# One SBUF layout for all layers of a two-layer decoder trunk, and output projections that take half of their k-tiles by seven-product blocks

## The chip, the cores and the metric

The kernel runs on one core of a Trainium2 chip. The core has a matrix engine (TensorE, PE in the profile, with PEld for its weight loads), a vector engine (VectorE, DVE), an activation engine (ScalarE, ACT), GpSimd (POOL), and SyncE (SP), whose queue issues the weight loads from device memory. On-chip memory is SBUF, 128 partitions wide; TensorE writes its sums to PSUM, eight banks of 512 float32 columns per partition.

The metric is the device time of one execution in microseconds, the median of several runs. Less is better.

## The reference

The program computes a decoder trunk of two layers on 256 positions and a width of 2048, all in float32:

```
def reference(x, ...):
    for layer in range(2):
        h = rms_norm(x, mix_norm[layer])
        if layer is even:
            z, xbc, dt_raw, c_q, c_kv, k_rope = split(h @ w_in)
            y_ssd = ssd_mixer(...)      # state space, 32 heads of 64, norm with a gate silu(z)
            y_mla = mla_mixer(...)      # latent attention, 16 heads of 128
            mix = concat(y_ssd, y_mla) @ w_out_even        # (4096, 2048)
        else:
            q, k, v = split(h @ w_qkv)
            mix = stick_breaking(q, k, v) @ w_out_odd      # (2048, 2048), 16 heads of 128
        x = x + mix
        h = rms_norm(x, ffn_norm[layer])
        x = x + (silu(h @ w_gate) * (h @ w_up)) @ w_down   # hidden width 5632
    return rms_norm(x, final_norm)
```

What matters here are the three square projections of 2048 to 2048 that write into the residual `x`: the upper half of `w_out_even` (from the state-space heads), its lower half (from the latent attention heads, MLA), and `w_out_odd` (from the stick-breaking heads).

## The kernel before, in words

**Products.** A float32 number is split in two parts, hi (a cast to the matrix engine's float32r) and lo (the rest). A product of two matrices is three matmuls: hi by hi, lo by hi, hi by lo. The cast is ACT's (`split`, L251), the subtraction that leaves lo is DVE's (L252). Each weight is loaded once into a tile of 4 k-tiles by 512 columns (1 MB), and split into two tiles wh and wl, called parts here.

**Plain projections.** `project` walks through the k-tiles of one block of 512 output columns; for each k-tile there are 3 matmuls for each of the two halves of the 256 positions (L345 to L347). A block over 16 k-tiles is 96 matmuls of 128x512. Two PSUM banks take the sums, and the next block uses the other two.

**Seven-product pairs.** `pair` computes two blocks at once: the gate's and the up-projection's 512 columns in the feed-forward stage. Its first 8 k-tiles form a 2x2 block product (two halves of the positions by two halves of k on one side, two halves of k by two column blocks on the other), taken by seven products in place of eight, after Winograd. A product is 12 matmuls (L499, L500, L504), so the phase of seven products has 84. The other 8 k-tiles are done in the plain way (96 matmuls, L532 to L534). For the seven products the weights are added to each other first (`wadd`, L470), and so are the activations (`block_operands`, L434, L447 and L448), once for a stage. In the text w11, w22, w21 are the splits of loaded weights, and wt1 to wt4 those of the four sums t1 to t4. The products use, in this order, w11, w22, wt1, w21, wt2, wt4, wt3. The lo part of a weight is used in the last four of the 12 matmuls only. DVE takes two more subtractions of the partial results (L515).

**Memory.** SBUF holds a pool of 42 tiles for activations (`s2`), three weight tiles, and one shared region that is laid out in two ways. In a mixing layer (`acts`) it holds 20 further activation tiles (`s2x`) and four parts each of wh and wl of two k-tiles. In a feed-forward stage (`sums`) it holds a fourth weight tile, three parts each of wh and wl of four k-tiles, and two tiles for sums. `region` changes from one to the other between the stages.

**Order.** The order of PE's instructions is written out by hand. Beside the projections stand small tasks (generators, `spawn`), which go on after so many ticks; a tick is one k-tile of a projection, or a half of a product. The heads of the attention, the state-space groups, transposes and the activations' splits are such tasks; `join` runs a task to its end where its result is needed. DVE, ACT, POOL and SP are put in order by a scheduler, by priority among what it holds to be ready: weight loads, weight splits and weight sums have priorities that count up from 100000, urgent work has 50000, and the rest, at 10000000 and up, comes last.

The even layer runs: the convolution's input projections with the state-space groups beside them, the latent projections, four blocks of the gate z, four MLA groups, then the state-space half of the output projection, then MLA's half. The odd layer runs four groups of stick-breaking heads, then its output projection.

Of the kernel before, what the change touches and what calls it, by code (L numbers as in the profile page):

```python
# [8 lines left out]
F32 = mybir.dt.float32  # L9
# [6 lines left out]
P = 128  # L16
D = 2048
KD = D // P
# [9 lines left out]
class Trunk:  # L28
# [6 lines left out]
    def __init__(self, ctx, tc, ins, out):  # L35
# [5 lines left out]
        self.ap = ec(tc.tile_pool(name="acts", bufs=42))  # L41
# [4 lines left out]
        self.shared, self.shared_kind = None, None  # L46
        self.region("acts")
        ctx.callback(self.region, None)
        self.banks = ["acc0", "acc1", "acc2", "acc3"]
        self.n = self.wn = 0  # L50
# [37 lines left out]
    def region(self, kind):  # L88


        if self.shared is not None:
            self.shared.__exit__(None, None, None)
        self.shared, self.shared_kind = None, kind
        if kind:
            self.shared = self.tc.tile_pool(name=f"shared_{kind}", bufs=2, reuse_waits="tile")
            self.xp = self.shared.__enter__()

    def s2x(self, shape, dt=F32):

        return self.xp.tile([P, *shape], dt, name=self.nm("s2x"), tag="s2x", bufs=20)  # L100
# [12 lines left out]
    def wsum(self):  # L113
        return self.xp.tile([P, 4, 512], F32, name=self.nm("wsum"), tag="wsum", bufs=2)
# [27 lines left out]
    def constants(self):  # L142
# [14 lines left out]
        with self.priority(self.wprio + 6500):  # L157
            self.wdt = []
            for q in range(4):
                w = self.s2x([4, 96])  # L160
# [141 lines left out]
    def load_split(self, view, nk, n):  # L302

        nc = self.nc
        for k0 in range(0, nk, 4):
            k1 = min(nk, k0 + 4)
            res = []
            with self.priority(self.wprio):
# [7 lines left out]
                np = 2 if self.shared_kind == "acts" else 4  # L316
                for a in range(k0, k1, np):
                    b = min(k1, a + np)
                    wh, wl = self.part("wh"), self.part("wl")
                    step = 1 if self.wprio < 102000 else np  # L320
                    for c in range(0, b - a, step):
                        d = min(c + step, b - a)
                        self.split(wh[:, c:d, :n], wl[:, c:d, :n], w[:, a - k0 + c:a - k0 + d, :n])
                    for k in range(a, b):
                        res.append((wh[:, k - a, :n], wl[:, k - a, :n]))
# [58 lines left out]

    def norm_begin(self):
        return {"ssq": self.small([P, 2, 4], "ssq"), "xT": [], "A": [], "S": []}
# [8 lines left out]
    def add_residual(self, ps, j, scale=None):  # L395
        nc, x = self.nc, self.xres
        for t in range(2):
            xs = x[:, t, j * 512:(j + 1) * 512]
            with self.priority(self.URGENT):
                if scale is None:  # L400
                    nc.vector.tensor_tensor(xs, ps[t], xs, op=ALU.add)
                else:
                    nc.vector.scalar_tensor_tensor(xs, ps[t], scale[:, t:t + 1], xs, op0=ALU.mult, op1=ALU.add)
# [4 lines left out]
    def operand_block(self, st, j, g):  # L408

        nc, x = self.nc, self.xres

        def gen():
            for t in range(2):
                yield 2 if t == 0 else 1
                pt = self.tr([4, P])
                for k in range(4):
                    nc.tensor.transpose(pt[:, k], x[:, t, j * 512 + k * P:j * 512 + (k + 1) * P], self.ident)
                r = self.s2([4, P])  # L420
                nc.vector.tensor_tensor(r, pt, g[:, 4 * j:4 * j + 4].unsqueeze(2).to_broadcast([P, 4, P]),
                                        op=ALU.mult)
                st["A"].append(r)
            for t in range(2):
                self.square_sum(x[:, t, j * 512:(j + 1) * 512], st["ssq"][:, t, j:j + 1])
            if j == 1:
                yield 1
                st["S"].extend(self.block_operands(*st["A"]))
        st["xT"].append((self.spawn(gen()), None))

    def block_operands(self, a11, a21, a12, a22):

        nc = self.nc
        sub = lambda o, p, q: nc.vector.tensor_tensor(o, p, q, op=ALU.subtract)  # L434
        d1, d2, d4 = (self.s2([4, P]) for _ in range(3))
        sub(d1, a21, a22)
        sub(d2, a11, d1)
        sub(a21, a21, a11)
        sub(d4, a12, d2)
        res = []  # L440
        for n, a in enumerate((a11, a12, a22, d1, d2, a21, d4)):
            hi, lo = self.s2([4, P], F32R), self.s2([4, P], F32R)
            if n == 0:
                nc.scalar.activation(hi, a, AF.Copy, scale=-1.0)
                nc.vector.scalar_tensor_tensor(lo, a, -1.0, hi.bitcast(F32), op0=ALU.mult, op1=ALU.subtract)
            else:
                nc.scalar.copy(hi, a)  # L447
                nc.vector.tensor_tensor(lo, a, hi.bitcast(F32), op=ALU.subtract)  # L448
            res.append((hi, lo))
        return res  # L450
# [16 lines left out]
    def wadd(self, o, p, q):  # L467
        with self.priority(self.wprio):
            self.wprio += 100
            self.nc.vector.tensor_tensor(o, p, q, op=ALU.add)  # L470
        return o

    def pair(self, st, xT, va, vb, left, right):
# [3 lines left out]
        mm = nc.tensor.matmul  # L477
        b11, b12 = self.wload(va, 0), self.wload(vb, 0)
# [77 lines left out]
    def ffn(self, layer, st, gain_next):  # L556
        nc, i = self.nc, self.i
        wg, wu, wd = i["w_gate"][layer], i["w_up"][layer], i["w_down"][layer]
        self.region("sums")
        xT, rstd = self.pairs(st["xT"]), None  # L560
        h = [None, None]

        def left(t, c, s):
# [3 lines left out]
            nc.vector.tensor_tensor(s, c, s, op=ALU.subtract)  # L567
# [9 lines left out]
        for nb in (2, 2, 2, 2, 3):  # L577
            act = []
            for n in range(n0, n0 + nb):
                self.pair(st, xT, self.cols(wg, n * 512), self.cols(wu, n * 512), left, right)  # L580
# [16 lines left out]
        if gain_next is not None:  # L597
            self.region("acts")
# [42 lines left out]
    def stick(self, st):  # L641
        nc, i = self.nc, self.i
        wq = i["w_qkv"][0]
        oT, xT, rstd = [], self.pairs(st["xT"]), None
        for g in range(4):
# [13 lines left out]
            oT.append((self.spawn(self.stick_out(v, ws, wts, res)), res))  # L659
        aT = self.pairs(oT)  # L660
        st = self.norm_begin()
        for n in range(4):
            ps = self.project(aT, self.cols(i["w_out_odd"][0], n * 512), KD)
            self.add_residual(ps, n)
            if n < 2:
                self.operand_block(st, n, self.g_ffn[1])
            else:
# [471 lines left out]
```

## Time and profile before

| what | value |
|---|---|
| median of 3 runs | 2493.59 us (2492.51 to 2496.81) |
| profiled execution | 2491.61 us, of which the span is 2489.9 us |
| PE busy | 2438.8 us (98%) |
| DVE busy | 1739.2 us (70%) |
| ACT busy | 1324.8 us (53%) |
| POOL busy | 127.7 us (5%) |

A line of the page or of a view names the line of the program, the engine, the operation, what it writes and reads, and the shapes. A group's line ends with busy time, the mean duration in ns, and the idle time of the engine before these instructions with what ended it. A line of the waits has the total, how often, and the longest. A line of the timeline has start and duration, and in brackets the idle time ahead of it. A line of the windows has a stretch from and to, its length, the busy time of PE, PEld, DVE, ACT and POOL (each with its number of instructions), the granted clock of PE, the share of the DMA engines, and GB/s. Matmuls overlap, so the duration of one (some 390 ns) isn't the step from one to the next.

### The profile page before, as it was taken

The page shows a single profiled execution, that of the slowest core. Times are in us where ns is not written, and L with a number is a line of the kernel's source. Part 1 is how long each engine was busy: PE and PEld are TensorE (multiplying, and loading weights), DVE is VectorE, ACT ScalarE, POOL GpSimd, SP SyncE. Part 2 cuts the span into 40 slices and gives each one's busy share as a digit, 9 for nine tenths or more (in the row PEclk, how much of TensorE's full clock was granted, in tenths as well). Part 3 has the DMA queues.
Part 4 walks back from the last instruction along what each step waited for, and adds up shares of the span by engine and source line. Part 5 has one row for each costly group of instructions (what it writes and reads, how often), then busy time and mean ns, then how long its engine had stood idle before and what let it go on. Part 6 is the DMA issues. An engine that isn't in the chain of part 4 may idle for free.

```text
span 2489.9 us, 28071 instructions
## 1 busy us (share of the span) xinstructions
PE 2438.8 (98%) x11176; PEld 2008.5 (81%) x11176; DVE 1739.2 (70%) x1631; ACT 1324.8 (53%) x1421; POOL 127.7 (5%) x165
## 2 busy tenths in 40 slices
PE   8989999999899999999999999999999999999998
PEld 7777887788778888888878888888778888888877
DVE  6776555546777878787984555556777878787874
ACT  6655555434554545454654456564554545554553
POOL 1342121000000000000000000000000000000001
PEclk9999999999999999999999999999999999999999
DMA  7554553355465656565654555555555656565653
GB/s 236 187 168 136 183 163 111 119 186 186 168 215 175 220 177 224 174 209 196 204 202 152 183 161 163 169 170 184 178 195 184 217 173 221 170 234 170 237 188 117
DMA packets 257828, 454.81 MB, mean 183 GB/s; under 512 B 20716, under 2 KB 45424, under 8 KB 257696
## 3 DMA queue, kind: packets, MB, share of 16 engines
q1 hardware_dynamic: 255168, 446.48, 54.3%
q0 software_dynamic: 1952, 5.48, 0.7%
q8 instruction: 88, 1.44, 0.2%
q10 hardware_dynamic: 576, 1.05, 0.1%
q14 instruction: 44, 0.36, 0.0%
HBM read 450.85 MB, written 2.13 MB: 182 GB/s over the span
## 4 chain that ended last, share of the span: by engine, by line
PE 60%; issue 34%; DVE 3%; POOL 1%; DMA 1%; ACT 1%; SPq 0%; POOLq 0%; ACTq 0%; DVEq 0%
PE acc L345 13%; PE acc L347 13%; PE acc L346 13%; PE acc L532 3%; PE acc L534 3%; PE acc L533 3%; PE acc L499 2%; PE acc L500 2%; PE acc L504 2%; DVE wl L252 1%; PE tr L261 1%; PE at L1062 1%; POOL s L967 1%; ACT wh L251 1%; PE at L991 1%
## 5 line engine op out<-in xcount | busy, mean ns | idle before, releaser
L252 DVE TENSOR_TENSOR wl<-w,wh 128x1024 fp32r<-128x1024 f32 (+2 forms) x586 | 997.7, 1709 | 553.1 <-ACT wh L251 549.1
L251 ACT CAST wh<-w 128x1024 fp32r<-128x1024 f32 (+2 forms) x586 | 837.1, 1430 | 788.2 <-PE acc L347 531.9
L345 PE MATMUL acc<-wh,s 128*128 128x512 f32 (+1 forms) x1728 | 692.2, 401 | 0.6 <-ACT wh L251 0.6
L346 PE MATMUL acc<-wl,s 128*128 128x512 f32 (+1 forms) x1728 | 671.5, 389 | 1.8 <-DVE wl L252 1.7
L347 PE MATMUL acc<-wh,s 128*128 128x512 f32 (+1 forms) x1728 | 672.4, 389 | 0.0
L347 PEld LDWEIGHTS acc<-wh,s 128*128 128x128 f32 x1728 | 325.4, 188 | 68.9
L346 PEld LDWEIGHTS acc<-wl,s 128*128 128x128 f32 x1728 | 326.5, 189 | 66.0 <-DVE wl L252 2.8
L345 PEld LDWEIGHTS acc<-wh,s 128*128 128x128 f32 x1728 | 326.4, 189 | 63.6 <-issue 2.4
L534 PE MATMUL acc<-wl,s 128*128 128x512 f32 x704 | 274.1, 389 | 0.0
L532 PE MATMUL acc<-wh,s 128*128 128x512 f32 x704 | 273.9, 389 | 0.0
L533 PE MATMUL acc<-wh,s 128*128 128x512 f32 x704 | 273.9, 389 | 0.0
L499 PE MATMUL acc<-wh,s 128*128 128x512 f32 x616 | 245.4, 398 | 0.0
L500 PE MATMUL acc<-wh,s 128*128 128x512 f32 x616 | 242.2, 393 | 0.0
L504 PE MATMUL acc<-wl,s 128*128 128x512 f32 x616 | 166.9, 393 | 12.3 <-DVE wl L252 12.3
L251 ACT CAST wh<-wsum 128x2048 fp32r<-128x2048 f32 x66 | 126.4, 1915 | 87.3 <-PE acc L533 33.7
L252 DVE TENSOR_TENSOR wl<-wsum,wh 128x2048 fp32r<-128x2048 f32 x66 | 150.7, 2286 | 13.5 <-ACT wh L251 13.5
L534 PEld LDWEIGHTS acc<-wl,s 128*128 128x128 f32 x704 | 132.1, 188 | 28.2 <-DVE wl L252 0.8
L533 PEld LDWEIGHTS acc<-wh,s 128*128 128x128 f32 x704 | 132.1, 188 | 27.4
L532 PEld LDWEIGHTS acc<-wh,s 128*128 128x128 f32 x704 | 132.1, 188 | 27.4
L504 PEld LDWEIGHTS acc<-wl,s 128*128 128x128 f32 x616 | 115.7, 189 | 39.2 <-DVE wl L252 15.3
L499 PEld LDWEIGHTS acc<-wh,s 128*128 128x128 f32 x616 | 117.8, 191 | 23.6
L500 PEld LDWEIGHTS acc<-wh,s 128*128 128x128 f32 x616 | 117.4, 191 | 23.5
(247 smaller groups left out, 2057.8 us busy)
## 6 DMA issues: line engine op xcount, KB each, us to landing
w<-in_w_gate_dram SPq DMA_DIRECT2D x88, 1024.0 KB, 5.1
w<-in_w_up_dram SPq DMA_DIRECT2D x88, 1024.0 KB, 5.1
w<-in_w_down_dram SPq DMA_DIRECT2D x88, 1024.0 KB, 5.0
w<-in_w_qkv_dram SPq DMA_DIRECT2D x48, 1024.0 KB, 5.0
w<-in_w_in_dram SPq DMA_DIRECT2D x47, 1024.0 KB, 5.1
w<-in_w_out_even_dram SPq DMA_DIRECT2D x32, 1024.0 KB, 4.9
w<-in_w_out_odd_dram SPq DMA_DIRECT2D x16, 1024.0 KB, 4.9
w<-in_w_ukv_dram SPq DMA_DIRECT2D x32, 256.0 KB, 3.8
```

Source lines behind the costliest of these rows:

```text
L251: nc.scalar.copy(hi, src)
L252: nc.vector.tensor_tensor(lo, src, hi.bitcast(F32), op=ALU.subtract)
L261: self.nc.tensor.transpose(pt[:, k, t * P:(t + 1) * P], src(t, 2 * k2 + k), self.ident)
L345: nc.tensor.matmul(ps[t], hi[:, ts], wh, start=k == 0, stop=False)
L346: nc.tensor.matmul(ps[t], hi[:, ts], wl, start=False, stop=False)
L347: nc.tensor.matmul(ps[t], lo[:, ts], wh, start=False, stop=k == nk - 1)
L499: mm(ps, hi[:, k], wh[:, k], start=start and k == 0, stop=False, skip_group_check=True)
L500: mm(ps, lo[:, k], wh[:, k], start=False, stop=False, skip_group_check=True)
L504: mm(ps, hi[:, k], wl[:, k], start=False, stop=k == 3, skip_group_check=True)
L532: mm(ps, hi, wh, start=False, stop=False, skip_group_check=True)
L533: mm(ps, lo, wh, start=False, stop=False, skip_group_check=True)
L534: mm(ps, hi, wl, start=False, stop=stop, skip_group_check=True)
```

## The change

All layers use one layout of SBUF: 46 activation tiles, four weight tiles, three parts each of wh and wl of four k-tiles, and one tile for sums. `region`, `s2x` and the two-k-tile parts go.

With one tile for sums, `pair` writes the sums t1, t2 and t4 into the same tile, each after the one before it has been split; the signs of the sums are another choice, which needs no negated activations.

The three output projections go through `pair` (`project_residual`): two pairs of column blocks for each. Their first 8 k-tiles (two groups of heads) are kept as plain tiles and become the seven operands (`operand_ready`); the other two groups are split as before.

In the even layer the state-space half of the output projection comes ahead of the MLA groups, not behind them. The state-space task waits 6 ticks in place of 3 ahead of the matmul of the chunk's state.

```diff
-        self.ap = ec(tc.tile_pool(name="acts", bufs=42))
+        self.ap = ec(tc.tile_pool(name="acts", bufs=46))
...
-    def wtile(self):
-        self.wn += 1
-        pool, bufs = (self.xp, 1) if self.shared_kind == "sums" and self.wn % 4 == 0 else (self.wp, 3)
-        return pool.tile([P, 4, 512], F32, name=self.nm("w"), tag="w", bufs=bufs)
+    def wtile(self, tag="w", dt=F32, bufs=4):
+        return self.wp.tile([P, 4, 512], dt, name=self.nm(tag), tag=tag, bufs=bufs)
...
     def part(self, tag):
-        nk, bufs = (2, 4) if self.shared_kind == "acts" else (4, 3)
-        return self.xp.tile([P, nk, 512], F32R, name=self.nm(tag), tag=tag, bufs=bufs)
-
-    def wsum(self):
-        return self.xp.tile([P, 4, 512], F32, name=self.nm("wsum"), tag="wsum", bufs=2)
+        return self.wtile(tag, F32R, 3)
...
+    def project_residual(self, st, view, scale=None, done=None):
+        def add(n):
+            def take(t, c, s):
+                if s is not None:
+                    nc.vector.tensor_tensor(s, c, s, op=ALU.add)
+                    c = s
+                self.add_tile(t, c, n, scale() if scale else None)
+            return take
+        for n in (0, 2):
+            self.pair(st, view(n), view(n + 1), add(n), add(n + 1))
+            if done:
+                done(n)
+                done(n + 1)
...
+    def operand_ready(self, st, j, res):
+        nc = self.nc
+        st["A"][j] = res
+        if len(st["A"]) < 2:
+            return
+        (a11, a21), (a12, a22) = st["A"][0], st["A"][1]
+        s1, s2, s4 = (self.s2([4, P]) for _ in range(3))
+        sub = lambda o, p, q: nc.vector.tensor_tensor(o, p, q, op=ALU.subtract)
+        nc.vector.tensor_tensor(s1, a21, a22, op=ALU.add)
+        sub(s2, s1, a11)
+        sub(a21, a11, a21)
+        sub(s4, a12, s2)
+        for a in (a11, a12, a22, s1, s2, a21, s4):
+            hi, lo = self.s2([4, P], F32R), self.s2([4, P], F32R)
+            self.split(hi, lo, a)
+            st["S"].append((hi, lo))
...
-        t1 = self.wadd(self.wsum(), b11, b12)
+        t = self.wtile("wsum", bufs=1)
+        self.wsub(t, b12, b11)
         w11 = self.wsplit(b11)
-        t2 = self.wadd(self.wsum(), t1, b22)
-        t3 = self.wadd(b12, b12, b22)
         w22 = self.wsplit(b22)
-        wt1 = self.wsplit(t1)
-        t4 = self.wadd(self.wsum(), t2, b21)
+        wt1 = self.wsplit(t)
+        self.wsub(t, b22, t)
         w21 = self.wsplit(b21)
-        wt2, wt4, wt3 = self.wsplit(t2), self.wsplit(t4), self.wsplit(t3)
+        self.wsub(b12, b22, b12)
+        wt2 = self.wsplit(t)
+        self.wsub(t, b21, t)
+        wt4, wt3 = self.wsplit(t), self.wsplit(b12)
...
-        for n in range(4):
-            ps = self.project(aT, self.cols(i["w_out_odd"][0], n * 512), KD)
-            self.add_residual(ps, n)
+        self.project_residual(oT, lambda n: self.cols(i["w_out_odd"][0], n * 512), None,
+                              lambda n: self.norm_next(st, n, self.g_ffn[1]))
...
+    def out_tiles(self, g):
+        if g < 2:
+            return [self.s2([4, P]) for _ in range(2)]
+        return [(self.s2([2, S], F32R), self.s2([2, S], F32R)) for _ in range(2)]
...
+        wo = i["w_out_even"][0]
+        self.project_residual(uT, lambda n: self.cols(wo, n * 512), lambda: r_u)
+        oT = self.operand()
         for g in range(4):
             self.mla_group(g, self.pairs(cT[:1]), self.pairs(cT[1:]), oT)
...
-        yield 3
+        yield 6
         pst = self.at([512])
```

More of the change, by code (lines that the diff above doesn't have):

```diff
@@ L418, in gen @@
                 for k in range(4):
-                    nc.tensor.transpose(pt[:, k], x[:, t, j * 512 + k * P:j * 512 + (k + 1) * P], self.ident)
+                    nc.tensor.transpose(pt[:, k], src(t, k), self.ident)
                 r = self.s2([4, P])
[L421 to L425, printed above, removed]
@@ L558, in ffn @@
         wg, wu, wd = i["w_gate"][layer], i["w_up"][layer], i["w_down"][layer]
-        self.region("sums")
-        xT, rstd = self.pairs(st["xT"]), None
+        rstd = None
         h = [None, None]
@@ L1019, in mla_group, with done @@
         v = self.evac(self.project(ckv, heads(wkv, 128, 128), 4))
-        o = [(self.s2x([2, S], F32R), self.s2x([2, S], F32R)) for _ in range(2)]
-        tasks = [self.spawn(self.mla_head(h, qp, q, k, v, o, 2 + 4 * h)) for h in range(4)]
-        oT.append((self.spawn(self.wait_all(tasks)), o))
+        o, left = self.out_tiles(g), [0, 1, 2, 3]
+        def done(h):
+            left.remove(h)
+            if g < 2 and not left:
+                self.operand_ready(oT, g, o)
+        tasks = [self.spawn(self.mla_head(h, qp, q, k, v, g, o, 2 + 4 * h, done)) for h in range(4)]
+        oT["xT"].append((self.spawn(self.wait_all(tasks)), o))
     def wait_all(self, tasks):
```

171 lines of the change are left out of this document (76 added, 95 removed).

## The prediction

> **What bounds the kernel now.** I read the page's first part, the waits of PE, the windows of the seven-product blocks, and the timeline of one of them.
>
> ```profile
> span 2489.9 us, 28071 instructions
> PE 2438.8 (98%) x11176; PEld 2008.5 (81%) x11176; DVE 1739.2 (70%) x1631; ACT 1324.8 (53%) x1421; POOL 127.7 (5%) x165
> PE acc L504 <- DVE wl L252: 12.3, 6, 3.4
> PE at L983 <- POOL s L980: 10.1, 3, 3.4
> PE tr L261 <- DVE s L575: 9.9, 4, 2.9
> ```
>
> PE is hardly ever idle, so a matmul removed is time gained, and so is a wait of PE: the three rows are nearly all of them. A new wait of PE is time lost in full. The windows below are the seven-product phases (84 matmuls) of some pairs in the feed-forward stages: length, then busy time of PE, PEld, DVE, ACT.
>
> ```profile
> 652.70:682.10 29.40, 22.54 (x93) 17.40 (x92) 29.36 (x24) 20.77 (x21) 0.00 (x0) 0.94 0.34 110
> 704.20:728.20 24.00, 21.57 (x93) 17.60 (x93) 21.87 (x14) 16.02 (x12) 0.00 (x0) 0.93 0.44 140
> 921.70:940.60 18.90, 18.90 (x85) 15.64 (x84) 17.64 (x11) 14.75 (x10) 0.00 (x0) 1.00 0.43 131
> 962.50:982.40 19.90, 19.90 (x93) 16.49 (x92) 19.86 (x14) 15.83 (x12) 0.00 (x0) 1.00 0.40 119
> 1258.20:1280.40 22.20, 20.00 (x93) 16.33 (x92) 20.96 (x14) 16.02 (x12) 0.00 (x0) 1.00 0.43 141
> 1764.30:1793.70 29.40, 23.93 (x93) 18.66 (x92) 29.36 (x24) 20.75 (x21) 0.00 (x0) 0.88 0.45 145
> 1815.90:1840.40 24.50, 21.61 (x93) 17.62 (x92) 22.25 (x14) 16.02 (x12) 0.00 (x0) 0.93 0.44 145
> ```
>
> A clean phase takes 18.9 us after a projection and 19.9 us after another pair (8 transposes more); DVE works through nearly all of either. The first two pairs of each feed-forward stage are far longer. Here is the clean one of 921.7, beginning with its first two matmuls:
>
> ```profile
> 921.72 0.39 PE L499 MATMUL acc<-wh,s 128*128 128x512 f32 x1
> 921.92 1.92 ACT L251 CAST wh<-wsum 128x2048 fp32r<-128x2048 f32 x1 [3.52 <-PE acc L347]
> 921.95 0.39 PE L500 MATMUL acc<-wh,s 128*128 128x512 f32 x1
> 923.74 1.92 ACT L251 CAST wh<-w 128x2048 fp32r<-128x2048 f32 x1
> 923.87 2.29 DVE L252 TENSOR_TENSOR wl<-wsum,wh 128x2048 fp32r<-128x2048 f32 x1 [1.26 <-ACT wh L251]
> 926.08 2.28 DVE L252 TENSOR_TENSOR wl<-w,wh 128x2048 fp32r<-128x2048 f32 x1
> 926.46 1.92 ACT L251 CAST wh<-wsum 128x2048 fp32r<-128x2048 f32 x1 [0.33 <-PE acc L500]
> 928.28 2.28 DVE L470 TENSOR_TENSOR wsum<-wsum,w 128x2048 f32<-128x2048 f32 x1
> 930.49 2.28 DVE L252 TENSOR_TENSOR wl<-wsum,wh 128x2048 fp32r<-128x2048 f32 x1
> 930.66 1.92 ACT L251 CAST wh<-wsum 128x2048 fp32r<-128x2048 f32 x1
> 932.69 0.68 DVE L515 TENSOR_TENSOR s<-s,s 128x512 f32<-128x512 f32 x1
> 933.29 2.29 DVE L252 TENSOR_TENSOR wl<-wsum,wh 128x2048 fp32r<-128x2048 f32 x1
> ```
>
> Matmuls start 0.227 us apart (921.72 to 921.95), so a product of 12 takes 2.72 us. The split of wt1 (cast 921.92) begins only as the phase does: it waits for PE to release the third part (3.52 us, L347). t2 and t3 were summed before. Of the sums only t4 is left (928.28), and the cast of wt4, the sixth product's operand, starts at 930.66, 9.0 us into the phase.
>
> **The change, part by part.** S is the start of a phase.
>
> *Fewer matmuls.* Two column blocks took 192 matmuls and take 84+96 = 180. Three output projections have two pairs each: 6 x 12 x 0.227 = 16.3 us gained.
>
> *One sum buffer.* t2 is now written over t1 and t4 over t2. So t2 must wait for both halves of wt1's split, and t4 for both of wt2's. At the durations shown: wt1 cast S+0.2 to 2.1, its low half to 4.4; t2 to 6.7; DVE then does w21's low half to 9.0 while ACT casts wt2; wt2's low half to 11.2; the 0.68 subtraction (L515, urgent) to 11.9; t4 to 14.2; wt4's cast to 16.1. PE wants it after five products, S+13.6: a stall of 2.5 us. wt4's low half ends at 18.4, and is wanted 8 matmuls (1.8 us) after the product's start, at 17.9 or so: 0.5 more. I take **3.0 us** for 10 pairs that follow a projection in the feed-forward and all 6 new ones, and 3.7 for the 12 that follow a pair, where two urgent low halves of the transposed activations (686 ns each, the L252 s<-tr row below) enter the chain on DVE (less transposes that PE does meanwhile): 16 x 3.0 + 12 x 3.7 = 92 us lost. Bounds for each: 2.2, if nothing but the chain itself runs (1.9+2.3+2.3+1.9+2.3+2.3+1.9 = 14.9, so wt4 is cast at S+15.3, 1.7 late, and 0.5 as above), and 5.3, if DVE takes w21's low half ahead of t2, as it took it (926.08) ahead of t4 here. That buffers for inputs stay four, and b12 = b22-b12 can be done in the phase ahead, where the dropped t2 leaves room, I cost at nothing; without that room it is 2.28 on DVE, inside the upper bound.
>
> The Trainium skill, "Perfetto Trace Analysis", section Optimization Strategy, says that the same gap repeating on the engine that should be saturated can mean too few buffers for the next tile. No gap repeats in the steady phases shown; by it the chain would show as one that does.
>
> *The clock.* A stall can be followed by a stretch at half clock:
>
> ```profile
> 658.05:661.46 3.41, 3.41 (x10) 2.82 (x11) 3.41 (x2) 2.36 (x3) 0.00 (x0) 0.50 0.64 185
> 709.25:712.66 3.41, 3.12 (x11) 2.65 (x12) 3.41 (x4) 1.07 (x2) 0.00 (x0) 0.50 0.42 162
> 149.47:152.88 3.41, 3.41 (x8) 2.09 (x7) 0.00 (x0) 1.75 (x3) 1.69 (x4) 0.50 0.93 335
> 1263.30:1266.70 3.40, 3.39 (x19) 2.92 (x20) 3.40 (x3) 2.06 (x4) 0.00 (x0) 1.00 0.10 40
> 709.54 0.44 PE L261 MATMUL tr<-ident,s 128*128 128x128 f32 x1 [2.43 <-DVE s L575]
> ```
>
> The 3.4 us waits were followed by 3.41 us at 0.50, and so was the 2.43 us wait at 709.54; the one ahead of 1263.30, of the same kind, was not. So stalls of 2.5 sometimes cost half of 3.41, 1.7 us, more: 28 x 0.3 x 1.7 = 14 us (bounds 0 and 48).
>
> *State-space wait.* The pause ahead of the chunk-state matmul grows from 3 ticks to 6, some 18 matmuls or 4.1 us. The L983 row's three waits, 3.4 at the longest and 10.1 in all, fit in that; with a half-clock stretch after each (149.47) 10.1 + 3 x 1.7 = 15 us gained. POOL's work itself is not shortened; bounds 0 and 15.
>
> *Start of the feed-forward.* The region switch goes:
>
> ```profile
> 652.19 1.37 DVE L401 TENSOR_TENSOR xres<-acc,xres 128x512 f32<-128x512 f32 x2 [7.89 <-PE acc L347]
> 653.48 2.28 DVE L470 TENSOR_TENSOR wsum<-w,w 128x2048 f32<-128x2048 f32 x1
> ```
>
> DVE sat 7.9 us and summed its first weights only when PE had already entered the phase, since their memory was the old region's. The four long phases sum to 29.4+24.0+29.4+24.5 = 107.3 against 2 x 18.9 + 2 x 19.9 = 77.6 clean, plus 8 transposes each in the first two (2 x 1.0): 27.7, of which I take 27 (bounds 15 and 28). Their chains are in the 92. The two third pairs (1258.20, 22.2 us) lose some of their L575 wait, as the phase ahead has a sum less: 3 us gained (0 to 5).
>
> *Output pairs on DVE.* Their cover was slack of the projections.
>
> ```profile
> 921.70:962.40 40.70, 40.70 (x181) 33.70 (x180) 36.35 (x22) 24.35 (x17) 0.00 (x0) 1.00 0.62 207
> 563.00:652.00 89.00, 89.00 (x406) 73.68 (x405) 50.98 (x56) 41.36 (x53) 0.00 (x0) 1.00 0.58 195
> L252 DVE TENSOR_TENSOR s<-tr,s 128x512 fp32r<-128x512 f32 x44 | 30.2, 686 | 9.5 <-ACT s L251 9.5
> L421 DVE TENSOR_TENSOR s<-tr,va 128x512 f32<-128x512 f32 x8 | 5.5, 692 | 3.4 <-PE tr L419 3.4
> L448 DVE TENSOR_TENSOR s<-s,s 128x512 fp32r<-128x512 f32 x12 | 7.7, 684 | 0.0
> L401 DVE TENSOR_TENSOR xres<-acc,xres 128x512 f32<-128x512 f32 x88 | 59.1, 688 | 39.3 <-PE acc L347 39.3
> ```
>
> The old attention projection kept DVE busy 51 us of 89; a pair keeps it busy 36 of 41. In the second output pair ahead of each feed-forward fall the operands for the next one: 4 multiplies, 4 sums and 7 low halves at about 0.69, 10.4 us, and some 1.2 more of residual adds: 48 us of DVE in a pair of some 45 with its stalls. I take 4 us for each of the two places, 8 lost (bounds 0 and 25). The first pair also runs the last attention group's heads; a head whose result is late stops PE at the join on group 3, 22 ticks in. I count that in the upper bound. The activation casts and the changed signs are the same instructions: nothing.
>
> *Order and buffers.* With the state-space half ahead of MLA, its 16 weight loads on SP are queued ahead of MLA's, and MLA's last heads run beside the next pair instead. The weights have four 1 MB buffers instead of three in these stages, so SP loads no later. DVE and ACT split 2048 columns at once there, less time in all; idle anyway. But the 42 + 20 activation tiles become 46 for everything. At the stick-breaking stage 16 hold the input and 14 the operands, and a group's four heads want some 16: it just fits, late evictions cover by one projection (PE's two other banks). I take 3 us lost; bounds 0 and 30.
>
> Sum: -16.3 +92 +14 -15 -27 -3 +8 +3 = **+56 us** on 2491.6, the profiled execution (1.7 outside the span), so 2547. The median of the runs is 2.0 higher: **2549**.
>
> **The rivals.**
>
> *The chain is hidden (faster).* If the wt4 cast came by S+13.6, only gains stay: -61 + 8 + 3 = -50, 2443. For it: DVE's order is planned, and wt3's independent part could let wt1 in sooner. Against it: the 3.52 us wait of the cast for PE. It decides below 1.8 us a pair: 28 x 1.8 = 50.
>
> *Stall without clock loss.* The clock drops only after longer waits: 56 - 14, 2535. For it: nothing followed at 1263.30. Against: 709.25. The Trainium skill, "TensorE: Matmul & The Clock Gate", section HAM oscillation, gives the rule as no PE-idle gaps over about 3.4 us; by it 2.5 us stalls would leave the clock alone and this rival holds. The 2.43 us row speaks against the rule.
>
> *w21 first.* DVE puts w21's low half ahead of t2 in every pair: 28 x 2.3 = 64 more, and stalls near 5 us always cost the half clock, 28 x 0.7 x 1.7 = 33 more: 2646.
>
> *Starved of tiles.* Each of the state-space gate, MLA and stick-breaking stages makes PE wait an eviction, 10 us or more each: 27 over my 3, 2576 or above. For it: 62 tiles become 46. Against: heads are done one by one.
>
> **How the numbers follow.** Forecast 0.41; no clock loss 0.20; hidden chain 0.17; w21 first 0.10; starved 0.12. The forecast's own range, chain bounds 2.2 and about 4 with the clock from 0 to 30, is 2510 to 2595. The whole: down to 2455, part of the hidden chain, up to 2615, beyond the starved case. A measurement tells 0.2% (5 us) from no change. Faster 0.18 (hidden chain and the edge of the lower bounds), same 0.04, slower 0.78.
>
> **What would show it.** The phases after: 21.9 us instead of 18.9, with a wait of PE for ACT's wh (L499) about 2.5 us long at the sixth product, in some 28 places; PE at L983 without waits; no 29 us phase at a stage's start; output pairs 180 matmuls in about 44 us. If phases keep 18.9 us, the forecast is wrong from its largest term on.

## The result, and the profile after

The changed kernel takes 2617.93 us (median of 4 runs, 2615.82 to 2625.89), the kernel before 2494.68 in runs beside it (2492.51 to 2496.81): a ratio of 1.050, 95% interval 1.0476 to 1.0524. The forecast was 2549, its range ended at 2615. The span of the profiled execution grew from 2489.9 to 2614.1 us, by 124.

The head of the page of the changed kernel, and then the three largest of the waits of its PE (line, what was waited for, us in all, times, longest):

```profile
span 2614.1 us, 27629 instructions
PE 2473.8 (95%) x11104; PEld 2011.3 (77%) x11104; DVE 1844.7 (71%) x1561; ACT 1345.7 (51%) x1337; POOL 142.7 (5%) x165
```

```profile
PE acc L506 <- ACT wh L227: 72.7, 26, 3.6
PE acc L506 <- ACT s L517: 29.6, 10, 5.3
PE acc L511 <- DVE wl L228: 4.1, 19, 0.2
```

The 72 matmuls are gone (11176 to 11104), yet PE is busy 35 us longer, part of it because 102.4 us of the trace ran at half clock, and 27.3 before (without a stretch at the very end of each). The first wait is the one that the prediction named, for ACT's wh. The second is new, and the prediction has no term for it: L517 is `keep`, the copy by which ACT takes a product's partial result out of a PSUM bank that the next product but one writes again.

Windows of the seven-product phases of the changed kernel (length, then busy time of PE, PEld, DVE, ACT, POOL, then the granted clock). The first two are a feed-forward phase after a projection and one after a pair, which took 18.9 and 19.9 us before; the next three are phases of the new output pairs (MLA's two, and the second of stick-breaking); the last is one stretch in the first window:

```profile
803.30:828.00 24.70, 21.38 (x85) 16.66 (x84) 20.05 (x12) 15.26 (x11) 0.00 (x0) 0.93 0.31 97
849.80:875.40 25.60, 22.02 (x93) 17.48 (x92) 21.60 (x14) 16.24 (x13) 0.00 (x0) 0.93 0.30 94
544.00:580.90 36.90, 32.73 (x147) 24.39 (x145) 26.29 (x32) 22.33 (x32) 0.00 (x0) 0.95 0.39 132
607.50:642.30 34.80, 25.79 (x102) 20.41 (x101) 30.50 (x27) 21.52 (x26) 0.00 (x0) 0.85 0.31 103
1784.80:1820.20 35.40, 26.38 (x102) 20.85 (x101) 30.51 (x27) 21.65 (x26) 0.00 (x0) 0.81 0.31 99
821.43:824.84 3.41, 3.41 (x10) 2.62 (x9) 3.41 (x2) 3.41 (x3) 0.00 (x0) 0.50 0.59 229
```

A steady phase grew by 5.7 us, and the forecast had it grow by 3.0 with half a microsecond for the clock. Here is the phase of 803.3 in the timeline, DVE's and ACT's part of the chain and the matmul that waited for it:

```profile
803.52 1.92 ACT L227 CAST wh<-wsum 128x2048 fp32r<-128x2048 f32 x1 [3.53 <-PE acc L320]
805.47 2.29 DVE L228 TENSOR_TENSOR wl<-wsum,wh 128x2048 fp32r<-128x2048 f32 x1 [1.26 <-ACT wh L227]
807.68 2.29 DVE L228 TENSOR_TENSOR wl<-w,wh 128x2048 fp32r<-128x2048 f32 x1
809.88 2.29 DVE L471 TENSOR_TENSOR wsum<-w,wsum 128x2048 f32<-128x2048 f32 x1
812.26 1.91 ACT L227 CAST wh<-wsum 128x2048 fp32r<-128x2048 f32 x1
814.20 2.29 DVE L228 TENSOR_TENSOR wl<-wsum,wh 128x2048 fp32r<-128x2048 f32 x1 [1.21 <-ACT wh L227]
816.53 2.29 DVE L471 TENSOR_TENSOR wsum<-w,wsum 128x2048 f32<-128x2048 f32 x1
818.91 1.90 ACT L227 CAST wh<-wsum 128x2048 fp32r<-128x2048 f32 x1 [0.54 <-DVE wsum L471]
820.86 0.51 PE L506 MATMUL acc<-wh,s 128*128 128x512 f32 x1 [3.11 <-ACT wh L227]
```

Each row begins about when the one above has ended, from the cast of t1 (803.52) to the cast of t4 (818.91): the serial chain of the prediction. In one place it is longer: at 807.68 DVE takes w21's low half, and t2 only at 809.88. PE waits 3.11 us, and 0.57 us after it resumes the clock falls to 0.50 for 3.41 us.

By stages, from the first matmul of a phase to the next part, the 124 us lie so: the even layer up to its feed-forward +11.3 (652.7 to 664.0); the seven-product phases of the two feed-forward stages 232.2 to 276.9 and 232.9 to 278.2, +90.1; the odd layer's mixing, with the down-projections ahead of it, +19.9 (462.0 to 481.9); the rest, +3, in the feed-forward outside the phases. The state-space wait is gone: no wait of PE at L996 (L983 before), and its eight matmuls take 590 ns, where the median was 1042.

### The profile page after: what moved, and what is told of

Read it like the earlier page. It is cut to its first block, busy times and chain, and to the rows that moved or that the text cites. A ratio compares the mean times of both kernels' runs of the same rounds, so it can differ in the third digit from the quotient of the medians.

```text
span 2614.1 us, 27629 instructions
## 1 busy us (share of the span) xinstructions
PE 2473.8 (95%) x11104; PEld 2011.3 (77%) x11104; DVE 1844.7 (71%) x1561; ACT 1345.7 (51%) x1337; POOL 142.7 (5%) x165
## 5 line engine op out<-in xcount | busy, mean ns | idle before, releaser
L228 DVE TENSOR_TENSOR wl<-w,wh 128x2048 fp32r<-128x2048 f32 (+2 forms) x431 | 966.9, 2254 | 501.0 <-ACT wh L227 500.6
L227 ACT CAST wh<-w 128x2048 fp32r<-128x2048 f32 (+2 forms) x431 | 802.8, 1873 | 679.2 <-PE acc L320 347.5
L318 PE MATMUL acc<-wh,s 128*128 128x512 f32 (+1 forms) x1600 | 637.5, 398 | 0.7 <-ACT wh L227 0.7
L320 PE MATMUL acc<-wh,s 128*128 128x512 f32 (+1 forms) x1600 | 621.8, 389 | 0.0
L319 PE MATMUL acc<-wl,s 128*128 128x512 f32 (+1 forms) x1600 | 620.6, 388 | 0.1
L506 PE MATMUL acc<-wh,s 128*128 128x512 f32 x784 | 334.1, 426 | 102.3 <-ACT wh L227 72.7
L541 PE MATMUL acc<-wl,s 128*128 128x512 f32 x896 | 349.8, 390 | 1.3 <-DVE wl L228 1.1
L540 PE MATMUL acc<-wh,s 128*128 128x512 f32 x896 | 348.9, 389 | 1.5 <-DVE s L228 1.5
L539 PE MATMUL acc<-wh,s 128*128 128x512 f32 x896 | 349.4, 390 | 0.0
L320 PEld LDWEIGHTS acc<-wh,s 128*128 128x128 f32 x1600 | 300.7, 188 | 63.0
L319 PEld LDWEIGHTS acc<-wl,s 128*128 128x128 f32 x1600 | 301.5, 188 | 57.9 <-issue 1.2
L318 PEld LDWEIGHTS acc<-wh,s 128*128 128x128 f32 x1600 | 301.4, 188 | 57.9 <-issue 1.2
L507 PE MATMUL acc<-wh,s 128*128 128x512 f32 x784 | 323.9, 413 | 0.0
L506 PEld LDWEIGHTS acc<-wh,s 128*128 128x128 f32 x784 | 157.3, 201 | 153.8 <-ACT wh L227 86.5
L228 DVE TENSOR_TENSOR wl<-wsum,wh 128x2048 fp32r<-128x2048 f32 x84 | 192.5, 2292 | 95.6 <-ACT wh L227 95.6
L227 ACT CAST wh<-wsum 128x2048 fp32r<-128x2048 f32 x84 | 160.3, 1908 | 172.4 <-DVE wsum L471 89.9
L511 PE MATMUL acc<-wl,s 128*128 128x512 f32 x784 | 225.8, 412 | 4.1 <-DVE wl L228 4.1
L541 PEld LDWEIGHTS acc<-wl,s 128*128 128x128 f32 x896 | 168.2, 188 | 39.3 <-DVE wl L228 4.6
L540 PEld LDWEIGHTS acc<-wh,s 128*128 128x128 f32 x896 | 168.3, 188 | 36.7 <-DVE s L228 2.0
L539 PEld LDWEIGHTS acc<-wh,s 128*128 128x128 f32 x896 | 168.3, 188 | 34.6
L511 PEld LDWEIGHTS acc<-wl,s 128*128 128x128 f32 x784 | 155.4, 201 | 48.0 <-DVE wl L228 14.4
L507 PEld LDWEIGHTS acc<-wh,s 128*128 128x128 f32 x784 | 157.7, 201 | 31.2
```

Source lines behind the costliest of these rows:

```text
L227: nc.scalar.copy(hi, src)
L228: nc.vector.tensor_tensor(lo, src, hi.bitcast(F32), op=ALU.subtract)
L318: nc.tensor.matmul(ps[t], hi[:, ts], wh, start=k == 0, stop=False)
L319: nc.tensor.matmul(ps[t], hi[:, ts], wl, start=False, stop=False)
L320: nc.tensor.matmul(ps[t], lo[:, ts], wh, start=False, stop=k == nk - 1)
L506: mm(ps, hi[:, k], wh[:, k], start=start and k == 0, stop=False, skip_group_check=True)
```

## The experiments

Every kernel ran beside the kernel before on the same chip (medians 2493.05 to 2495.49). Where no interval is given, it was one run. The theory was that the chain through the single sum tile makes up most of the loss. The rivals: the order on DVE (w21 first), the fewer activation tiles, and the output pairs.

**The chain taken apart.** t2 is formed as b11 + t3 in the tile of b11, ahead of the phase, and t4 is summed straight from it into the one sum tile as soon as t1's split has left it. Still one sum tile and 46 activation tiles:

```diff
...
         self.wsub(t, b12, b11)
         w11 = self.wsplit(b11)
+        self.wsub(b12, b22, b12)
+        self.wadd(b11, b11, b12)
         w22 = self.wsplit(b22)
         wt1 = self.wsplit(t)
-        self.wsub(t, b22, t)
+        t4 = self.wtile("wsum", bufs=1)
+        self.wsub(t4, b21, b11)
         w21 = self.wsplit(b21)
-        self.wsub(b12, b22, b12)
-        wt2 = self.wsplit(t)
-        self.wsub(t, b21, t)
-        wt4, wt3 = self.wsplit(t), self.wsplit(b12)
+        wt2 = self.wsplit(b11)
+        wt4, wt3 = self.wsplit(t4), self.wsplit(b12)
```

> The changed kernel with one edit in the pair: t2 is formed as b11 + t3 in b11's own weight tile, ahead of the phase, so that it no longer waits for the split of t1; still one sum tile, which t4 takes over from t1. Theory A (the chain of wt1's split, t2, wt2's split, t4 and wt4's cast through one tile makes the 5.8 us that each seven-product phase has gained): the 22 feed-forward phases go back to 18.9 and 19.9 us, 126 us less, and the 6 output phases lose up to 5.8 us each, so 2457 to 2490 us; no wait of PE for wh at the sixth product, and no half clock in the feed-forward. Theory B (46 activation tiles in place of 62 starve the stages): the output phases of 34 to 37 us stay as they are, and the time falls by the feed-forward's part at most, or not at all. Theory C (the phases are long since DVE has too much work in all): DVE's work is the same, so the time stays at 2618 us.

It took 2502.03 us, a ratio to before of 1.0032 (1.0019 to 1.0044). So the chain costs 2617.9 - 2502.0 = 116 us, and the time is still 12 us above the range expected. The feed-forward phases are back at 19.0 and 20.0 us, but for the first (25.9 and 27.4) and the last (24.0) of each stage; the rest of the loss isn't the chain. The list of PE's waits in this kernel shows where it lies; the window of MLA's second output phase and its timeline (ACT and the matmuls that waited, at 631.55 and, the two rows ahead, at 556.80) show why:

```profile
PE acc L512 <- ACT s L523: 33.3, 13, 4.7
PE tr L237 <- DVE s L587: 4.7, 3, 2.2
```

```profile
612.00:641.10 29.10, 22.80 (x102) 18.25 (x101) 27.98 (x26) 21.31 (x26) 0.00 (x0) 0.94 0.44 147
```

```profile
...
555.81 0.37 ACT L1095 ACTIVATE s<-at,mx 128x128 f32<-128x128 f32 x1 [2.44 <-DVE mx L1093]
...
556.80 0.79 PE L512 MATMUL acc<-wh,s 128*128 128x512 f32 x1 [4.17 <-ACT s L523]
...
626.00 1.90 ACT L227 CAST wh<-w 128x2048 fp32r<-128x2048 f32 x1 [0.20 <-PE acc L513]
627.81 3.21 ACT L227 CAST s<-s 128x512 fp32r<-128x512 f32 x6
630.92 0.57 ACT L523 COPY s<-acc 128x512 f32<-128x512 f32 x1
631.55 0.79 PE L512 MATMUL acc<-wh,s 128*128 128x512 f32 x1 [4.74 <-ACT s L523]
```

The copy L523 (L517 in the change) is urgent, and yet at 630.92 ACT does it last, after a weight cast and six casts of the next operands. PE waits 4.74 us for it. It has one product, 2.72 us, to get through. ACT is busy 21.3 us of these 29.1: it isn't full, it is late at one point. At 556.80 it is 4.17 us, behind a head's exponential (L1095), which itself waited for DVE. Of the ten others six are of 1.6 us, behind one weight cast, in two places with a head's exponential after it.

**Two sum tiles for four activation tiles.** The sums have a tile more, as before, and the activations 42:

```diff
-        self.ap = ec(tc.tile_pool(name="acts", bufs=46))
+        self.ap = ec(tc.tile_pool(name="acts", bufs=42))
...
-        t = self.wtile("wsum", bufs=1)
-        self.wsub(t, b12, b11)
+        t1 = self.wtile("wsum", bufs=2)
+        self.wsub(t1, b12, b11)
         w11 = self.wsplit(b11)
+        t2 = self.wtile("wsum", bufs=2)
+        self.wsub(t2, b22, t1)
...
+        t4 = self.wtile("wsum", bufs=2)
+        self.wsub(t4, b21, t2)
```

> The changed kernel with two sum tiles, as before the change, paid with four activation tiles (42 for 46). Theory A (the chain through one tile): feed-forward phases of 18.9 and 19.9 us, as with t2 in b11. Theory B (too few activation tiles): with four less, the stages of the mixing layers get longer, the output phases above 37 us, or waits come up in the attention groups; the difference to the run with t2 in b11 is what four tiles are worth. 2460 to 2490 us by A, 2620 or more by B.

2513.92 us: the steady feed-forward phases are clean again, 104 us below the change, but 12 above the kernel with one sum tile, and above the 2460 to 2490 expected. Its list of PE's waits has two of the mixing stages that are shorter there (2.0 for L272) or missing (POOL at L237):

```profile
PE acc L508 <- ACT s L519: 34.8, 14, 4.7
PE tr L237 <- POOL s L789: 5.5, 2, 2.8
PE tr L261 <- ACT s L272: 3.6, 2, 3.5
```

The four tiles between 42 and 46 are worth some 12 us in this one run, if the other way of forming t2 is worth nothing; 6 of them are lost ahead of the first output pair (it begins at 333.7 us, and at 327.6 with 46 tiles), where nothing is summed. The rival "starved of tiles" asks for 46 against the 62 of before, and the experiment with plain output projections below answers that.

**The order on DVE alone.** w21's split is issued behind t2; the chain stays:

```diff
...
-        self.wsub(t, b22, t)
-        w21 = self.wsplit(b21)
+        t2 = self.wsub(t, b22, t)
+        with self.tc.issue_after(t2.ins):
+            w21 = self.wsplit(b21)
```

> The changed kernel, in which w21's low half is queued behind t2 on DVE: the order that the prediction reckoned with. If the order was all that was wrong with the size: PE's wait at the sixth product falls from 3.3 and 3.7 us to about 2.5, a phase from 24.7 to some 22 to 23 us, 28 x 2 = 56 us less, about 2560. If the half clock that follows each wait is the larger part, it stays after 2.5 us waits too, and phases only fall to 24 us: 2600. If the wait is not set by this chain, nothing changes: 2618.

2586.09 us, 32 less than the change and 84 more than without the chain. DVE in a phase after a projection, then the matmul that waited there and in a later phase (timeline), the waits of PE, and the windows of these two phases:

```profile
809.64 2.29 DVE L228 TENSOR_TENSOR wl<-wsum,wh 128x2048 fp32r<-128x2048 f32 x1 [1.26 <-ACT wh L227]
811.97 2.29 DVE L471 TENSOR_TENSOR wsum<-w,wsum 128x2048 f32<-128x2048 f32 x1
814.18 2.28 DVE L228 TENSOR_TENSOR wl<-w,wh 128x2048 fp32r<-128x2048 f32 x1
823.73 0.50 PE L507 MATMUL acc<-wh,s 128*128 128x512 f32 x1 [2.47 <-ACT wh L227]
958.68 0.50 PE L507 MATMUL acc<-wh,s 128*128 128x512 f32 x1 [2.47 <-ACT wh L227]
```

```profile
PE acc L507 <- ACT wh L227: 53.6, 26, 2.6
```

```profile
807.50:829.70 22.20, 19.52 (x85) 15.53 (x84) 18.67 (x11) 15.00 (x11) 0.00 (x0) 1.00 0.32 97
942.40:965.70 23.30, 20.83 (x85) 16.70 (x85) 19.77 (x12) 14.95 (x11) 0.00 (x0) 0.93 0.34 100
```

With t2 ahead of w21 the wait is 2.47 us, the 2.5 of the prediction, and the phase 22.2, where the half clock stays away. The same wait comes with the half clock in one window and without it in the other.

**The pause of the state-space task alone, in the kernel before.**

```diff
-        yield 3
+        yield 6
```

> The kernel before, with the state-space pause of 6 ticks alone. Forecast of this step: the three waits of PE for POOL (10.1 us) and the half clock after them go, 15 us less, 2479. Its rival: POOL is as late for what follows, and the time stays at 2494.

2480.47 us, 12.6 below the kernel before beside it. No wait for POOL is left in PE's list.

**Plain output projections, with the chain taken apart.** The three output projections go back to 96 matmuls a block; with them goes the making of the seven operands in the mixing layers, and the rest is as in the first experiment:

```diff
-        for n in (0, 2):
-            self.pair(st, view(n), view(n + 1), add(n), add(n + 1))
+        for n in range(4):
+            ps = self.project(self.pairs(st["xT"]), view(n), KD)
+            for t in range(2):
+                add(n)(t, ps[t], None)
...
```

> The kernel with t2 in b11, with the three output projections done in the plain way again (four blocks of 96 matmuls each, hi and lo tiles for all four groups), in the new order and the new layout. Theory C (what is left of the loss after the sum chain, 9 us over the kernel before, comes from the pairs of the output projections, where PE waits for ACT's copy of the z bank behind casts and task work): 72 matmuls more (16 us), but the waits for that copy (33 us in 13 places) and their half clocks go: layer 0's eight blocks take some 180 us in place of 209, layer 1's four 90 in place of 105, and the first feed-forward phases stay near 20: 2455 to 2470. Theory B (46 tiles are too few): the layers stay long, 2495 or more.

2465.31 us, 0.9883 of before (0.9867 to 0.9900): faster than before, and 37 us faster than with the pairs, although 72 matmuls more are run. The odd layer's mixing takes 461.4 us with 46 tiles and took 462.0 with 62: it isn't starved. The profiled stages against the first experiment: even layer 650.4 instead of 663.1, odd mixing those 461.4 instead of 475.2, phases of the feed-forward 440.6 instead of 453.7. The loss by the pairs is in equal thirds, and one of them falls in the feed-forward stage, for the most part in its first phases, which had to wait for what the pairs had pushed back (25.9 and 27.4 us against 21.8). Some 29 of the 37 us can be counted: waits for the copy fell from 33.3 to 3.1 us, the time at half clock (but for the end) from 44.4 to 13.7, of which half is lost, and 16 go the other way for the matmuls. The rest is not accounted for.

**The operands' casts spread out.** The seven splits of the operands, one per tick instead of all at once:

```diff
+        def gen():
...
+            for a in (a11, a12, a22, s1, s2, a21, s4):
+                yield 1
...
+        st["op"] = self.spawn(gen())
...
+        self.join(st["op"])
```

> The kernel with t2 in b11, in which the seven splits of the activation operands come one a tick, not all at once. Theory C: the 4.7 us waits of PE for the copy of z behind six casts (two places), and the half clock after them, go: 2 x 6.4 = 13 us less, some 2489; the waits of 1.6 us behind one weight cast stay. If the total work of ACT or DVE in these phases is the limit and not the place of the copy in ACT's queue, the wait appears elsewhere and the time stays at 2502.

2505.79 us, no gain over 2502.03. PE's list:

```profile
PE acc L517 <- ACT s L528: 28.0, 14, 2.8
PE at L1090 <- DVE s L263: 6.2, 1, 6.2
```

The longest wait for the copy fell from 4.7 to 2.8 us, but their sum only from 33.3 to 28.0, and a wait of 6.2 came up elsewhere. The burst isn't the cause by itself: the waits of 1.6 us behind one weight cast stay.

**The order of the even layer.** From the kernel with plain outputs, the state-space half back behind MLA:

```diff
         wo = i["w_out_even"][0]
-        self.project_residual(uT, lambda n: self.cols(wo, n * 512), lambda: r_u)
         oT = self.operand()
         for g in range(4):
...
+        self.project_residual(uT, lambda n: self.cols(wo, n * 512), lambda: r_u)
```

> The kernel with plain output projections, with the state-space half behind MLA, as before the change. If the order of the two is worth nothing by itself: within 4 us of the run with the state-space half ahead. If the tiles held through MLA (16 for the state-space output) starve a pool of 46: PE waits in the MLA groups, 10 us or more longer.

2455.25 us; the same kernel in more runs:

> The kernel with t2 in b11, plain output projections, the state-space half behind MLA, the one layout and the pause of 6 ticks, for an interval: 2455, 1.5% faster than before. Its parts by the runs so far: some 13 us from the pause, the rest from the starts of the feed-forward stages without a region switch (29.6 and 24.1 to 21.8 and 20.0 us a stage).

2454.83 us, 0.9843 of before (0.9830 to 0.9857). So the new order costs 10 us, more than the 4 that would have meant nothing, and it wasn't the tiles held through MLA: with the old order and 46 tiles the even layer takes 638.7 us, and with 62, in the kernel before with the longer pause, 637.7. With the state-space half ahead, MLA's last heads have no projection left to stand beside; these rows of the kernel with plain outputs, from PE's list and its timeline, are gone with the old order, and so are 13.65 us at half clock that begin at 565.1:

```profile
PE at L1099 <- ACT s L1095: 3.2, 3, 2.0
PE tr L1093 <- DVE s L1089: 2.6, 1, 2.6
```

```profile
562.81 0.70 PE L1099 MATMUL at<-s,s 128*128 128x256 f32 x2 [2.04 <-ACT s L1095]
```

**No tasks inside the seven products.** On top of the spread operands, the two ticks of each product are taken out, so that no head or operand work stands between their matmuls:

```diff
-                if k == 1:
-                    self.tick()
...
-            self.tick()
```

> The kernel with spread operands, and no task goes on within the seven products: tasks go on in the plain half of a pair and in projections alone. Theory C: all 28 phases come to 19 us, without a wait for the copy of z; what the tasks took shows in the plain halves, as waits at the joins on the last attention group and on the normed input, 5 to 15 us in four places. 2470 to 2510.

2528.28 us, above the 2470 to 2510 expected. The waits went to where the tasks now pile up and are joined. The longest, 4.1 to 7.4 us, are in the products themselves: in MLA's first output phase and in the first phase of each feed-forward stage the low halves of the operands come late (L518). The others are in the plain halves (L548) and in the heads (L1111):

```profile
PE acc L518 <- DVE s L228: 18.4, 3, 7.4
PE acc L548 <- DVE s L248: 8.7, 4, 3.8
PE at L1111 <- ACT s L1107: 4.8, 5, 1.8
```

Of the feed-forward phases, though, all but the first of each stage are 19.0 us: in that stage ticks in the products only cost.

**The same in the feed-forward alone.** From plain outputs with MLA first, ticks in the products only in the first pair of a stage:

```diff
-    def pair(self, st, va, vb, left, right):
+    def pair(self, st, va, vb, left, right, tasks=True):
...
-                if k == 1:
+                if k == 1 and tasks:
                     self.tick()
...
-            self.tick()
+            if tasks:
+                self.tick()
...
-                self.pair(st, self.cols(wg, n * 512), self.cols(wu, n * 512), left, right)
+                self.pair(st, self.cols(wg, n * 512), self.cols(wu, n * 512), left, right, n == 0)
```

> The kernel with t2 in b11, plain output projections and the state-space half behind MLA, in which no task goes on within the seven products of the feed-forward, but for the first pair of each stage, which needs the normed input. The transposes (0.9 us a phase) only change their place; the waits of PE for DVE at the third pair of the last block (2.35 us, with a half clock at times) go: 2 x 3 to 2 x 5 us less than the run without this edit, 2445 to 2452. If the joins that follow make PE wait in the plain halves: 2455 or more.

2446.81 us, 0.9813 of before (0.9799 to 0.9826), the fastest. Phases of 21.8 us at the start of a stage, 19.0 after it. Its page and the first of PE's waits:

```profile
PE 2424.0 (99%) x11176; PEld 2000.2 (82%) x11176; DVE 1713.1 (70%) x1476; ACT 1298.8 (53%) x1266; POOL 133.8 (5%) x165
```

```profile
PE acc L513 <- ACT s L525: 3.1, 2, 1.6
```

**The chain with plain outputs.** From the kernel with plain outputs, the sums as the change has them:

```diff
-        self.wsub(b12, b22, b12)
-        self.wadd(b11, b11, b12)
...
-        t4 = self.wtile("wsum", bufs=1)
-        self.wsub(t4, b21, b11)
+        self.wsub(t, b22, t)
...
+        self.wsub(b12, b22, b12)
+        wt2 = self.wsplit(t)
+        self.wsub(t, b21, t)
+        wt4, wt3 = self.wsplit(t), self.wsplit(b12)
```

> The kernel with plain output projections, state-space half ahead, and t2 again in the one sum tile as the change has it. If the sum chain and the output pairs cost each for itself: the 22 phases of the feed-forward take 24.6 to 25.7 us as in the changed kernel, 2465 + 22 x 5.7 - some start-up = 2560 to 2590. If the chain is only as long as it is because the output pairs leave DVE behind: phases near 22 us, about 2520.

2580.74 us. PE waits 72.3 us in 22 places for wh, once in each phase of the feed-forward, and a phase (the window) has the length that it has in the change:

```profile
PE acc L512 <- ACT wh L227: 72.3, 22, 3.6
```

```profile
787.90:812.60 24.70, 21.37 (x85) 16.54 (x84) 20.05 (x12) 15.21 (x11) 0.00 (x0) 0.93 0.33 96
```

In their sum, chain and pairs don't depend on each other: the chain costs 2617.9 - 2502.0 = 116 us with the pairs and 2580.7 - 2465.3 = 115 without them, the pairs 37 with either. Phase by phase they do: without the pairs all 22 phases of the feed-forward grow, by 116 us in all; with them these grow by 101 (453.7 to 555.2) and the six output phases by 11 (177.9 to 188.8), as the first phases of a stage and the output phases have waits of their own already.

The whole path, from medians and single runs: 2494 before; -13 by the pause; -26 by one layout and no region switch (2480.5 to 2454.8); +10 by the order of the even layer (to 2465.3); +37 by the output pairs (to 2502.0); +116 by the chain (to 2617.9).

## Why the prediction was wrong

Its sign held, and so did the mechanism of its largest term: the one sum buffer costs more than all the rest brings. The size was 68 us short (+56 against +124), most of it by the output pairs, where it had the wrong engine. By its steps:

- *One sum buffer and the clock*, +92 and +14, together 106: measured 116, which is so close in part by luck, as two errors lie in it against each other. At the order that the step assumed, t2 ahead of w21, the chain costs 84 (2586.1 - 2502.0), with the forecast wait, 2.47 against 2.5; the step had 21 us for the six output phases, where even the change lost 11. But **DVE took w21's low half first**, after a projection and after a pair, as it took it ahead of t4 in the kernel before; that is 32 us more. It was the rival with 0.10, and priced at 97: it held, at a third of its price, because the wait became 3.1 to 3.6 us and not near 5. Adding the 2.3 us of w21's low half in full was the mistake: it is in the chain in either order. Put first, it no longer runs beside the cast of wt2 (1.9 us), but then the 0.68 subtraction does; the sixth product starts 17.54 us into the phase (803.32 to 820.86), and with t2 first 16.23 (807.50 to 823.73), so 1.3 are added. The lower bound has a slip too: 0.2 + 14.9 is 15.1 and not 15.3, which makes it 2.0 in place of 2.2. In the second pair of each feed-forward stage t2 did go first.
- The clock alone: in the trace of the change 102.4 us run at half clock, 27.3 before. Half of the difference, 38 us, is lost; the term was 14. Of the 18 waits of 3.1 to 3.6 us in the feed-forward 15 came with a stretch at 0.50, four of these 6.8 us long, while the term had 0.3 of them.
- *Fewer matmuls* and *output pairs on DVE*, -16 and +8: measured +37 together, so this is **the step that failed by most, 45 us**. It looked for the loss on DVE, whose work was counted against its slack; what stopped PE was ACT's queue, where the copy of a bank stands behind casts (33.3 us of waits in the first experiment), and each such wait can be followed by the half clock. The prediction wrote that the activation casts "are the same instructions: nothing". On ACT they aren't: the six output pairs bring 24 copies of a bank (L517 x112 in the change, L510 x88 before) and three more sets of operand casts. And a plain projection writes its next block into two other banks, so its next matmul doesn't wait for a copy. A late head did stop PE, as its sentence on the upper bound has it, but less at the join (1.5 us at 603.36 in the first experiment) than through the copy behind it (4.17 us at 556.80).
- *Order and buffers*, +3: the order alone was +10 (e.g. the waits at L1093 and L1099 above). That MLA's last heads "run beside the next pair instead" was right, and what stands beside it is not a cover: PE waits for the heads' steps (L1093, L1099). The tiles were no cost that shows, so the rival of starved stages is excluded at 46; 42 instead of 46 cost up to 12.
- *State-space wait*, -15: -13, right, with the wait gone from the list.
- *Start of the feed-forward* and third pairs, -27 and -3: measured -26 for one layout, with the sums as in the first experiment. The start phase fell from 29.6 to 21.8 us with plain outputs, which the step had; in the change, with output pairs ahead and the chain, it is 26.7.

So 106 became 116, -8 became +37, 3 became 10, -15 became -13 and -30 became -26: 10 + 45 + 7 + 2 + 4 = 68. The phases that were to show it, 21.9 us, are those of the kernel with t2 first, without the half clock (22.2); the output pairs of 44 us took 45 to 64 (the longest also run MLA's heads). Of the rivals "the chain is hidden" is excluded, "stall without clock loss" by the half clock in 15 places of 18.

Not settled: why the same wait of 2.47 us has the half clock behind it in some places and not in others, and why the scheduler takes w21 ahead of t2 in some phases and behind it in others. The pairs weren't tried with a copy that goes to another engine or bank, which might keep their 72 matmuls.

## What to carry to other kernels

A temporary that is reused in place turns independent sums into a chain over two engines; if the saturated engine needs its end within a fixed time, add up the chain first, and then see whether an input that is dead already can take one of the sums, which was worth 116 us here without another tile. Saved matmuls are worth 0.227 us each only where the block that saves them has its helpers free: its copies need a place in a queue within one product, so look at the queue of that engine and not at its share of busy time. A cover that is moved away from a step (MLA's last heads) is a cost, even where the moved work is unchanged.

## What the runs showed of the hardware that was not expected

The clock fell after shorter waits of PE (2.20 us at 1265.47 in the first experiment), and more often, than the prediction had it. In the feed-forward of the change, the eight waits of 3.10 to 3.12 us all came with half clock, of ten of 3.57 to 3.60 us seven, of four of 2.45 to 2.65 us none; with t2 first, 12 of 20 of 2.34 to 2.65 us. In four of the eight the stretch was twice as long, and began while PE still waited:

```profile
959.19 0.80 PE L506 MATMUL acc<-wh,s 128*128 128x512 f32 x1 [3.12 <-ACT wh L227]
```

```profile
958.00:964.80 6.80, 5.61 (x13) 4.45 (x14) 5.63 (x3) 6.54 (x4) 0.00 (x0) 0.50 0.47 155
```

In the fastest kernel the longest wait behind the first 10 us is 1.6 us, and no half clock is in its trace before its end. The Trainium skill, "TensorE: Matmul & The Clock Gate", section HAM oscillation, gives the rule as no PE-idle gaps over about 3.4 us. The traces here don't agree: half the clock was lost after 2.47 us (958.68, with t2 first) and after 3.11 us (820.86, the change), and not after three waits of 3.57 to 3.60 in the change; the length of the wait alone doesn't decide.
